# Both score maps of a head issued as one pair, attention spread over 13 and 14 gate units, and three smaller re-orderings in a two-layer backbone kernel

## The chip, the cores and the metric

The kernel runs on one core of one Trainium2 chip. The metric is the device time of one execution in microseconds (us), of which the kernel before has three timed runs. One further execution was recorded by the hardware profiler, and all rows below are from that one.

## The reference

A trunk of two layers works on 256 latent tokens and 256 context tokens of width 1024. Each layer has a mixer (differential attention beside a bidirectional state space, each gated, merged and projected) and a squared-ReLU MLP, both with RMSNorm ahead and behind. Cut to what the change touches:

```python
def diff_attend(q, k, v, lam):                    # two softmax maps per head
    s = einsum('bqhcd,bkhcd->bhcqk', q, k) * (HEAD_DIM_A ** -0.5)
    p = softmax(s, axis=-1)
    pd = p[:, :, 0] - lam * p[:, :, 1]            # their difference weights the values
    return einsum('bhqk,bkhe->bqhe', pd, v)

def trunk_layer(x, xc, ...):
    h = rmsnorm(x, norm_g[0]) * (1 + sc1) + sh1
    q, k, v, u, g = split(h @ w_in)               # latent q sees context and latent keys
    pa = (rmsnorm(latent_diff_attention(q, k_all, v_all, lam), subln_g) * (1 - lam_init)) @ w_br_a
    y_lat, y_ctx = s5_bidirectional(u, uc, ...)   # scans over tokens, then a readout
    y = gelu(y_lat); ps = (y * sigmoid(y @ w_glu + b_glu)) @ w_br_s
    ga, gs = split(sigmoid(g + gate_b))
    x = x + gt1 * rmsnorm((ga * pa + gs * ps) @ w_out, norm_g[1])
    h2 = rmsnorm(x, norm_g[2]) * (1 + sc2) + sh2
    x = x + gt2 * rmsnorm(square(relu(h2 @ w_mlp1 + b_mlp1)) @ w_mlp2 + b_mlp2, norm_g[3])
    # layer 0 does the same for the context tokens, whose queries see context keys only
```

There are 4 heads of two 64-wide maps with values 128 wide. Everything is float32.

## The kernel before

Layer 0 (L0) carries four tiles of 128 tokens (`nt=512` columns), layer 1 (L1) only the two latent ones (`nt=256`). Weights come in pieces of 512 KB on the DMA queue of SP into five buffers `raw`. ScalarE (ACT) rounds a piece to a high part `whi` (L145), VectorE (DVE) takes the rest as `wlo` (L147), and `mm3` (L151 to L153) multiplies in three matmuls, high by high, high by low and low by high.

**Order.** Each engine works through its own list of instructions in order, and a scheduler writes these lists from the order in the program, from buffers that come free and from ties of "issue order" that the program sets with `after(op, prev)`. While the 16 gate projections `ga` run on TensorE (PE), small work is spread between them: steps of the attention, of the scan, of the adaptive-norm product `ada`. `AJ[L]` says over how many of the gate projections the attention steps are spread. The same loop loads the readout matrices `M` (`mload`) and ends with the first pieces of the readout `y`.

**Attention.** One step takes a token tile and a head. `att1` makes for each of the two maps a score matmul `S` (L951: rows 0 to 63 or 64 to 127 of the array, into one of two banks `bbank`), its row maximum `mx` on DVE (L952) and its exponential on ACT (L954), and then the weighted difference `p` (L959). `att2`, one step later, transposes `p` (`pdt`, L966), copies that to `pdT` on ACT (L968) and multiplies with the values into `o` (L970). `att3` ends a token tile: squares, `rsq`, the scaled `on`, its transposes `ot` (L987), then `of` and `oh`. There are 24 such heads: 8 of 256 keys and 8 of 512 in L0, 8 of 512 in L1.

**Readout.** `ssm_out` builds the kernel matrices `kt` per group chunk and stores them to DRAM (`kd`), from where `M` is read back as overlapping windows (L1077). `ygen` multiplies `U` with `M` and the states `S_...` with `CLs` into `y`. `gelu` transposes `y` (`yt`, L1117), then Square, Tanh and the split into `ygh` (L1130) and `ygl`, which the matmuls `glu` take.

**Ends.** `pa_unit` projects the attention output (`pa`). `tail` ends a sub-layer per token tile: a product `mo`, its sum of squares, the multiply with the gate `g2` (L604), `rsq`, the residual `x` (L621), again sums of squares, `xn` (L634 on ACT, L636 on DVE), and behind the next tile's first matmuls the transposes `ht`.

Of the kernel before, what the change touches and what calls it, by code (L numbers as in the profile page):

```python
# [9 lines left out]
F32 = mybir.dt.float32  # L10
# [4 lines left out]
OP = mybir.AluOpType  # L15
# [23 lines left out]
TL = True  # L39
AJ = [14, 16]  # L40
SJ = [15, 10]
# [36 lines left out]
def trunk(tc, I, out):  # L78
    nc = tc.nc
    ctx = ExitStack()  # L80
    with ctx:
# [53 lines left out]

        nosync = mybir.DependencyInfo(mybir.DependencyClass.NoSync, mybir.DependencyReason.DATA)
        hold = {}

# [191 lines left out]
        def ssm_params(L):  # L330
# [125 lines left out]
            ssmt[L]["cl"] = [dram.tile([128, 8, 2, 128], F32, name=f"cl{L}_{c}") for c in range(4)]  # L456
            ssmt[L]["kd"] = [dram.tile([16, 8, 240], F32, name=f"kd{L}_{c}") for c in range(4)]
            yield
# [60 lines left out]
        def ssm_out(L, c):  # L519
# [12 lines left out]
            for g2, r, j, d in np.ndindex(2, 2, 4, 2):  # L532
# [3 lines left out]
                          start=(r == 0), stop=(r == 1), tile_position=(64 * d, 32 * j))  # L536
            kt = chk.tile([128, 2, 240], F32, name="kt")
            pf, pb_ = (p[:, 0:256].rearrange("p (g n) -> p g n", g=2) for p in pks)
# [7 lines left out]
            for j in range(4):  # L546
                S.dma_start(out=z["kd"][c][:, j:j + 5:4], in_=kt[32 * j:32 * j + 16])
            z["done", c] = True
# [33 lines left out]
        def tail(L, n, load, mm, evac, gg, store, norm, ks, fill, hk=None, before=None):  # L582


            late = None
            for t in range(n):
# [9 lines left out]
                def first(n, lo, hi, ps):  # L596
                    a = evac(t, lo, hi, ps)
                    sumsq(a, ss[:, n:n + 1])
                    if n == 0:
                        V.tensor_scalar(ss[:, 4:5], ss[:, 0:1], 1.0 / D, EPS, op0=OP.mult, op1=OP.add)  # L600
                    else:
                        V.scalar_tensor_tensor(ss[:, 4 + n:5 + n], ss[:, n:n + 1], 1.0 / D, ss[:, 3 + n:4 + n],
                                               op0=OP.mult, op1=OP.add)
                    V.tensor_tensor(a, a, g2[:, v, lo:hi], op=OP.mult)  # L604
                    rt.append((a, slice(lo, hi)))
# [12 lines left out]
                with hp(0):  # L618
# [12 lines left out]
                    for q in range(2):  # L631
                        sl = slice(q * 512, q * 512 + 512)
                        if XNE[q]:
                            A.activation(xn[:, sl], x[:, sl], AF.Copy, scale=r)  # L634
                        else:
                            V.tensor_scalar(xn[:, sl], x[:, sl], r, None, op0=OP.mult)  # L636

# [157 lines left out]
        for L in range(DEPTH):  # L795
# [147 lines left out]
            def att1(t, nk, h):  # L943
                qc = (t - t0) * 128
                mx = small.tile([128, 2], F32, name="mx", tag="mx")
                lsum = small.tile([128, 2], F32, name="lsum", tag="lsum")
                pp = []
                for m in range(2):
                    ps = bbank("S")
                    rr = slice(64 * m, 64 * m + 64)  # L950
                    PE.matmul(ps[:, :nk], qT[rr, h, qc:qc + 128], kT[rr, h, 0:nk], start=True, stop=True)  # L951
                    V.tensor_reduce(mx[:, m:m + 1], ps[:, :nk], axis=AX.X, op=OP.max, negate=True)  # L952
                    p = m2(nk, name="p")
                    A.activation(p, ps[:, :nk], AF.Exp, bias=mx[:, m:m + 1], accum_out=lsum[:, m:m + 1])  # L954
                    pp.append(p)
# [6 lines left out]
            def att2(t, nk, h, p, po):  # L962
# [6 lines left out]
                for j in range(nkt):  # L969
                    PE.matmul(po[:, h * 128:(h + 1) * 128], pd[:, j * 128:(j + 1) * 128],  # L970
                              Vk[:, j, h * 128:(h + 1) * 128], start=(j == 0), stop=(j == nkt - 1))

# [97 lines left out]
            def mload():  # L1070

                while ("done", 3) not in z:
                    pump()
                q = len(Ms)
                M = (slot([1024], name="M") if q == 3 and last else xtile("M"))
                kd = z["kd"][q]
                after(S.dma_start(out=M, in_=bass.AP(tensor=kd.tensor, offset=kd.offset,  # L1077
                                                     ap=[[16, 8], [240, 128], [1, 128]])), hold["raw"])
                Ms.append(M.rearrange("p (g n) -> p g n", g=8))

            def ygen():
# [9 lines left out]
                for b in range(8 // A_):  # L1091
# [3 lines left out]
                    for gi, r, a in np.ndindex(4, 3, A_):  # L1095
                        g = b * 4 * A_ + 4 * a + gi
                        if r == 0:
                            w, mv = U[:, g, 64 - ncol:64], Ms[g // 8][:, g % 8]
                        else:
# [9 lines left out]
            def gelu(bp, tq):  # L1109
# [6 lines left out]
                for t in range(4):  # L1116
                    PE.transpose(pt.rearrange("p (a t c) -> p t a c", a=A_, t=4)[:, t],  # L1117
                                 ysb[0][:, bp, 4 * tq + t].rearrange("p b h -> p (b h)"), ident)

# [36 lines left out]

            def pa_unit(fp):
                u = unit(L, U_GA + 3 * fp)
                for b in range(2):
                    k = 2 * fp + b  # L1160
                    pa = proj(u, lambda j: oh[:, j], lambda j: ol[:, j], 0, nt, kn=4, b=b, name="pa")
                    V.scalar_tensor_tensor(m1(k), m1(k), 1.0, pa[:, :nt], op0=OP.add, op1=OP.mult)

            if last:
                while len(ytasks) > 2:
                    ytasks.pop(0)()
                pump(PY[L])
                pa_unit(0)
                pump(PY[L])
                while ytasks:  # L1170
                    ytasks.pop(0)()
                pa_unit(1)
# [290 lines left out]
```

## Time and profile before

| what | value |
|---|---|
| timed runs | 1302.22 us (median of 3, 1299.68 to 1303.11) |
| the profiled execution's own time | 1297.54 us |
| its span (first to last instruction) | 1295.8 us |
| TensorE (PE) busy | 1227.7 us, 95% |
| VectorE (DVE) busy | 887.0 us, 68% |
| ScalarE (ACT) busy | 565.2 us, 44% |
| mean granted TensorE clock | 0.986 of full speed |
| moved by DMA | 228.62 MB, mean 176 GB/s |

The table is read from the top: how far the span is filled by one engine, then the others. Idle time of PE is 1295.8 less 1227.7, that is 68.1 us in the whole span.

### The profile page before, as it was taken

Reading aid. Unit: us, or ns where it says so; the run is one execution under the profiler, and the core shown is the slowest. Engines: PE = TensorE matmul, PEld = TensorE weight load, DVE = VectorE, ACT = ScalarE, POOL = GpSimd, SP = SyncE. Lnnn points to the kernel's source line nnn. Section 1 sums busy time; section 2 is a strip of 40 time slices with the busy share of each in tenths; the row PEclk is TensorE's granted clock in tenths of the full one; section 3 lists DMA queues with packets and bytes.
Section 4 is the critical chain, followed back from the end, with each engine's and each line's share of the span. In section 5 each row is a group of like instructions: output and inputs, shape, how many; then the busy total and the mean of one; then the engine's idle time right before and its main releaser. Section 6 shows DMA issues by size and latency. Waiting matters only on the chain.

```text
span 1295.8 us, 20541 instructions
## 1 busy us (share of the span) xinstructions
PE 1227.7 (95%) x8028; PEld 994.6 (77%) x8028; DVE 887.0 (68%) x2012; ACT 565.2 (44%) x992; POOL 0.2 (0%) x4
## 2 busy tenths in 40 slices
PE   6989999998899999999999999899997988999997
PEld 4668767666678877888778888786775886999996
DVE  7699888434576847987964456733887567766666
ACT  5423355446343642243232253523454644655453
POOL 0000000000000000000000000000000000000000
PEclk9999999999899999999999999999998999999999
DMA  9533372626743466244453243568527955465552
GB/s 372 203 127 114 117 267 82 174 70 237 267 150 143 156 226 213 83 161 154 171 199 93 81 158 120 190 212 335 184 83 196 345 182 180 171 199 180 190 189 81
DMA packets 76497, 228.62 MB, mean 176 GB/s; under 512 B 15952, under 2 KB 26864, under 8 KB 71920
## 3 DMA queue, kind: packets, MB, share of 16 engines
q1 hardware_dynamic: 68080, 225.21, 50.9%
q10 hardware_dynamic: 8320, 2.10, 0.7%
q8 instruction: 63, 1.03, 0.3%
q14 instruction: 34, 0.28, 0.1%
HBM read 205.29 MB, written 21.99 MB: 175 GB/s over the span
## 4 chain that ended last, share of the span: by engine, by line
PE 79%; DMA 8%; DVE 8%; ACT 3%; issue 1%; SPq 1%; DVEq 0%; ACTq 0%
PE m1p L151 6%; PE m1p L153 6%; PE m1p L152 6%; PE m2p L151 5%; PE m2p L152 5%; PE m2p L153 5%; PE mo L151 3%; PE mo L152 3%; PE mo L153 3%; DMA raw<-in_wts 3%; PE ga L151 3%; PE ga L152 2%; PE ga L153 2%; PE S L951 2%; PE ada L287 2%; DMA M<-kd 1%
## 5 line engine op out<-in xcount | busy, mean ns | idle before, releaser
L147 DVE TENSOR_TENSOR wlo<-raw,whi 128x1024 fp32r<-128x1024 f32 x206 | 251.4, 1222 | 166.8 <-ACT whi L145 162.2
L145 ACT ACTIVATE whi<-raw 128x1024 fp32r<-128x1024 f32 x206 | 217.5, 1060 | 335.9 <-PE m2p L153 99.9
L152 PE MATMUL m1p<-l,whi 128*128 128x512 f32 (+1 forms) x448 | 150.9, 337 | 0.0
L151 PE MATMUL m1p<-h,whi 128*128 128x512 f32 (+1 forms) x448 | 150.9, 337 | 0.0
L153 PE MATMUL m1p<-h,wlo 128*128 128x512 f32 (+1 forms) x448 | 150.8, 337 | 0.0
L152 PE MATMUL m2p<-wlo,hid 128*128 128x512 f32 x288 | 112.6, 391 | 0.0
L151 PE MATMUL m2p<-whi,hid 128*128 128x512 f32 x288 | 112.2, 394 | 0.0
L153 PE MATMUL m2p<-whi,hid 128*128 128x512 f32 x288 | 112.2, 390 | 0.0
L151 PE MATMUL ga<-hh,whi 128*128 128x512 f32 (+1 forms) x256 | 89.3, 349 | 4.5 <-ACT whi L145 4.5
L151 PEld LDWEIGHTS m1p<-h,whi 128*128 128x128 f32 x448 | 84.9, 190 | 10.5 <-issue 1.0
L152 PEld LDWEIGHTS m1p<-l,whi 128*128 128x128 f32 x448 | 84.9, 190 | 9.6 <-issue 0.2
L153 PEld LDWEIGHTS m1p<-h,wlo 128*128 128x128 f32 x448 | 85.0, 190 | 8.8 <-DVE kt L543 0.2
L153 PE MATMUL ga<-hh,wlo 128*128 128x512 f32 (+1 forms) x256 | 88.3, 346 | 0.6 <-DVE wlo L147 0.6
L152 PE MATMUL ga<-hl,whi 128*128 128x512 f32 (+1 forms) x256 | 88.3, 345 | 0.0
L151 PEld LDWEIGHTS m2p<-whi,hid 128*128 128x128 f32 x288 | 53.8, 188 | 13.6 <-issue 3.3
L153 PEld LDWEIGHTS m2p<-whi,hid 128*128 128x128 f32 x288 | 54.1, 188 | 11.2
L152 PEld LDWEIGHTS m2p<-wlo,hid 128*128 128x128 f32 x288 | 54.1, 188 | 10.4
L1282 ACT ACTIVATE hid<-zz 128x512 fp32r<-128x512 f32 (+1 forms) x64 | 33.2, 522 | 65.1 <-DVE zz L1281 65.1
L151 PEld LDWEIGHTS ga<-hh,whi 128*128 128x128 f32 x256 | 49.5, 193 | 15.4 <-issue 5.6
L1320 DVE TENSOR_TENSOR acc<-m2p,acc 128x512 f32<-128x512 f32 x60 | 40.9, 687 | 24.3 <-PE m2p L153 24.3
L153 PEld LDWEIGHTS ga<-hh,wlo 128*128 128x128 f32 x256 | 49.3, 193 | 10.6 <-issue 4.2
L152 PEld LDWEIGHTS ga<-hl,whi 128*128 128x128 f32 x256 | 49.5, 193 | 8.9 <-issue 4.5
(318 smaller groups left out, 2701.4 us busy)
## 6 DMA issues: line engine op xcount, KB each, us to landing
raw<-in_wts SPq DMA_DIRECT2D x227, 512.0 KB
raw<-in_ada_w SPq DMA_DIRECT2D x80, 512.0 KB
adaw<-in_ada SPq DMA_DIRECT2D x8, 1024.0 KB
cl<-CL SPq DMA_DIRECT2D x8, 1024.0 KB
CLs<-cl SPq DMA_DIRECT2D x8, 1024.0 KB
x<-in_x SPq DMA_DIRECT2D x8, 512.0 KB
M<-kd SPq DMA_DIRECT2D x8, 512.0 KB
et<-ET SPq DMA_DIRECT2D x4, 1024.0 KB
```

What stands on the lines that cost most here:

```text
L145: a = A.activation(hi, src, AF.Copy)
L147: after(eng.tensor_tensor(lo, src, f(hi), op=OP.subtract), hold.get("x"))
L151: after(PE.matmul(ps, sh, mh, start=first, stop=False), prev)
L152: PE.matmul(ps, sh, ml, start=False, stop=False)
L153: PE.matmul(ps, sl, mh, start=False, stop=last)
L287: PE.matmul(ps[32 * j:32 * j + 32, :n], cs[:, k, :], raw[:, o:o + n], start=(k == 0), stop=(k == 7))
L951: PE.matmul(ps[:, :nk], qT[rr, h, qc:qc + 128], kT[rr, h, 0:nk], start=True, stop=True)
L1282: A.activation(hi, zz, AF.Copy)
L1320: V.tensor_tensor(acc(ti, half), ps, bias2[:, half * 512:(half + 1) * 512] if grp == 0 else acc(ti, half), op=OP.add)
```

## The change

1. `AJ` goes from [14, 16] to [13, 14]: the attention steps end earlier among the gate projections.
2. In `att1` the two score matmuls of a head stand directly behind each other. The first waits for the last exponential of the head before (a real dependency) and stands behind the last `o` of the head before (issue order).
3. `kt` holds the two group halves interleaved, `kd` has the shape [16, 4, 480], a store writes pieces of 1920 bytes instead of 960, and `M` is read in 512 pieces of 1 KB instead of 1024 of 512 bytes. `y` reads every second element of such a tile.
4. In `tail` the multiply with the gate (L604) of a token tile stands behind the `xn` (L636) of the tile before on DVE.
5. In L1 the two `gelu` tasks stand between the halves b=0 and b=1 of `pa_unit(0)`.

```diff
-AJ = [14, 16]
+AJ = [13, 14]
...
-            ssmt[L]["kd"] = [dram.tile([16, 8, 240], F32, name=f"kd{L}_{c}") for c in range(4)]
+            ssmt[L]["kd"] = [dram.tile([16, 4, 480], F32, name=f"kd{L}_{c}") for c in range(4)]
...
-            kt = chk.tile([128, 2, 240], F32, name="kt")
+            ks = chk.tile([128, 480], F32, name="kt")
+            kt = ks.rearrange("p (n g) -> p g n", g=2)
...
-                S.dma_start(out=z["kd"][c][:, j:j + 5:4], in_=kt[32 * j:32 * j + 16])
+                S.dma_start(out=z["kd"][c][:, j], in_=ks[32 * j:32 * j + 16])
...
-                    V.tensor_tensor(a, a, g2[:, v, lo:hi], op=OP.mult)
+                    after(V.tensor_tensor(a, a, g2[:, v, lo:hi], op=OP.mult), normed)
...
-                            V.tensor_scalar(xn[:, sl], x[:, sl], r, None, op0=OP.mult)
+                            normed = V.tensor_scalar(xn[:, sl], x[:, sl], r, None, op0=OP.mult)
...
-                pp = []
+                pp, pss = [], []
                 for m in range(2):
                     ps = bbank("S")
                     rr = slice(64 * m, 64 * m + 64)
-                    PE.matmul(ps[:, :nk], qT[rr, h, qc:qc + 128], kT[rr, h, 0:nk], start=True, stop=True)
+                    o = PE.matmul(ps[:, :nk], qT[rr, h, qc:qc + 128], kT[rr, h, 0:nk], start=True, stop=True)
+                    if m == 0 and "exp" in hold:
+
+                        tc.add_manual_dep(o.ins, hold["exp"].ins.name, sync, reason="both banks")
+                        after(o, hold.get("o"))
+                    pss.append(ps)
+                for m, ps in enumerate(pss):
                     V.tensor_reduce(mx[:, m:m + 1], ps[:, :nk], axis=AX.X, op=OP.max, negate=True)
                     p = m2(nk, name="p")
-                    A.activation(p, ps[:, :nk], AF.Exp, bias=mx[:, m:m + 1], accum_out=lsum[:, m:m + 1])
+                    hold["exp"] = A.activation(p, ps[:, :nk], AF.Exp, bias=mx[:, m:m + 1], accum_out=lsum[:, m:m + 1])
...
-                                                     ap=[[16, 8], [240, 128], [1, 128]])), hold["raw"])
-                Ms.append(M.rearrange("p (g n) -> p g n", g=8))
+                                                     ap=[[32, 8], [480, 64], [1, 256]])), hold["raw"])
+                Ms.append(M.rearrange("p (j n g) -> p g j n", j=4, g=2))
...
+                    if between and b:
+                        between()
+                    pa = proj(u, lambda j: oh[:, j], lambda j: ol[:, j], 0, nt, kn=4, b=b, name="pa",
+                              prev=hold["yt"] if between and b else None)
...
-                pa_unit(0)
+
+                def gelus():
+                    while ytasks:
+                        ytasks.pop(0)()
+                pa_unit(0, gelus)
```

Each engine has as many instructions as before. What moves is their order; three places of PE's list and one of ACT's follow. A row is line, operation, output and inputs, and the columns of one matmul; "x2" is a row twice in succession.

**PE, a head of 512 keys in L0, before.** The gate projection runs on around it (`ga`), with `ada` work behind:

```order
L153 MATMUL ga<-hh,wlo 128x512
L951 MATMUL S<-kT,qT 128x512
L151 MATMUL ga<-hh,whi 128x512
L951 MATMUL S<-kT,qT 128x512
L152 MATMUL ga<-hl,whi 128x512
L970 MATMUL o<-Vk,pdT 128x128 x4
L153 MATMUL ga<-hh,wlo 128x512
L287 MATMUL ada<-raw,cs 32x256
L966 MATMUL pdt<-ident,p 128x128 x4
```

**The same engine, a head of 512 keys in L0, after** (lines are shifted by the edit: L953 is the score matmul, L978 `o`, L974 `pdt`):

```order
L154 MATMUL ga<-hh,wlo 128x512
L978 MATMUL o<-Vk,pdT 128x128 x4
L953 MATMUL S<-kT,qT 128x512 x2
L974 MATMUL pdt<-ident,p 128x128 x4
L288 MATMUL ada<-raw,cs 32x256 x8
L152 MATMUL ga<-hh,whi 128x512
```

The two scores stood apart and now stand together, behind the `o` of the head before the last and ahead of the `pdt` of the last. Over the whole list, 9 of the 24 heads had their scores side by side before (4 of 256 keys, 5 of 512) and 22 have now; all but the first head of each layer. Newly paired are 3 heads of 256 keys and 10 of 512. Between one pair and the next stand 25 rows or more in L0 from the sixth head on, mostly `ga`, but only `pdt` and `o` between the last two; in L1 there are 17 and 6 rows between three successive pairs, `ada`, `ot`, `pdt` and `o` among them, and 30 or more between the others.

**PE, L0, from the last `ot` of the attention to the readout's fourth bank, before:**

```order
L1101 MATMUL y<-CLs,S_3101 64x128
L987 MATMUL ot<-ident,on 128x128
L1117 MATMUL yt<-ident,ysb 128x2x64 x8
L305 MATMUL ada<-ident,row 128x128 x2
L1101 MATMUL y<-M,U 64x128 x2
L1101 MATMUL y<-CLs,S_3101 64x128 x4
```

**The same engine and place, after,** from the last `pa` ahead of that bank (20 further matmuls of `pa` stand between `yt` and these):

```order
L153 MATMUL pa<-ol,whi 128x512
L154 MATMUL pa<-oh,wlo 128x512
L306 MATMUL ada<-ident,row 128x128 x2
L152 MATMUL pa<-oh,whi 128x512
L153 MATMUL pa<-ol,whi 128x512
L154 MATMUL pa<-oh,wlo 128x512
L1109 MATMUL y<-M,U 64x128 x2
L1109 MATMUL y<-CLs,S_3101 64x128 x4
```

The bank that takes the last `M` stood right behind `yt`; now 25 `pa` matmuls of 512 columns stand ahead of it. The pieces of the other three banks keep their places.

**ACT, the turn of L1 from `y` to `glu`, before.** Each `whi` here rounds a weight piece into a buffer that a `pa` unit must first have read:

```order
L1103 ACTIVATE ysb<-y 128x4x8x16 x2
L145 ACTIVATE whi<-raw 128x1024
L1125 ACTIVATE yw<-yt 128x512 x2
L145 ACTIVATE whi<-raw 128x1024
L1128 ACTIVATE yw<-yw 128x512 x2
L145 ACTIVATE whi<-raw 128x1024
L1130 ACTIVATE ygh<-yg 128x4x128 x2
```

**The same engine and place, after:**

```order
L1111 ACTIVATE ysb<-y 128x4x8x16 x2
L1133 ACTIVATE yw<-yt 128x512 x2
L146 ACTIVATE whi<-raw 128x1024
L1136 ACTIVATE yw<-yw 128x512 x2
L146 ACTIVATE whi<-raw 128x1024
L1138 ACTIVATE ygh<-yg 128x4x128 x2
L146 ACTIVATE whi<-raw 128x1024
```

Each of the three `whi` stood ahead of a step of the GELU and now stands behind it; the one that waits for the last `pa` unit is behind `ygh`. On PE the eight `yt` stand behind 12 `pa` matmuls instead of 25, so 60 instead of 47 follow them ahead of `glu`.

Three smaller moves: in L1's `tail` DVE has the first tile's `xn` (L636) ahead of the second tile's two multiplies with the gate; in L1's gate projections `ot` of the first tile stands 1 us of work behind the last `o` instead of 32 `ga` matmuls; and the small loads `ab` and `gr` on SP stand behind five weight loads instead of ahead of them.

## Rows read from the trace of the kernel before

**Rows 1.** The page: the chain that ended last, share of the span by engine.

```profile
PE 79%; DMA 8%; DVE 8%; ACT 3%; issue 1%; SPq 1%; DVEq 0%; ACTq 0%
```

**Rows 2.** PE's waits: engine, instruction, releaser: us in total, times, longest.

```profile
PE y L1101 <- DMA M<-kd: 5.5, 1, 5.5
PE ga L151 <- ACT whi L145: 4.5, 2, 4.2
PE o L970 <- ACT pdT L968: 3.4, 3, 1.7
PE glu L151 <- ACT ygh L1130: 2.1, 1, 2.1
...
PE ot L987 <- ACT on L983: 1.7, 2, 1.4
...
PE S L951 <- ACT p L954: 0.5, 1, 0.5
```

**Rows 3.** Timeline of PE in L0 (start us, us, engine, line): a single score.

```profile
225.00 1.12 PE L951 MATMUL S<-kT,qT 64*128 64x512 f32 x2
226.06 0.50 PE L152 MATMUL ga<-hl,whi 128*128 128x512 f32 x1
```

**Rows 4.** Timeline in L0: a pair of scores (x4) and its chain.

```profile
218.06 1.13 PE L951 MATMUL S<-kT,qT 64*128 64x512 f32 x4
219.12 0.71 PE L970 MATMUL o<-Vk,pdT 128*128 128x128 f32 x4
...
221.15 0.69 ACT L954 ACTIVATE p<-S,mx 128x512 f32<-128x512 f32 x1
...
222.92 0.75 DVE L959 SCALAR_TENSOR_TENSOR p<-p,lsum 128x512 f32<-128x512 f32 x1
```

**Rows 5.** Timeline of PE in L0: a single score of 256 keys.

```profile
141.62 0.70 PE L951 MATMUL S<-kT,qT 64*128 64x256 f32 x2
142.24 0.50 PE L152 MATMUL v<-wlo,hh 128*128 128x512 f32 x1
```

**Rows 6.** Busy us by stretch: PE, PEld, DVE, ACT, POOL, granted clock, DMA share, GB/s.

```profile
200.00:227.00 27.00, 27.00 (x124) 19.75 (x123) 23.34 (x80) 14.11 (x31) 0.00 (x0) 1.00 0.25 79
321.00:328.00 7.00, 1.54 (x12) 1.23 (x14) 4.95 (x11) 3.46 (x7) 0.00 (x0) 0.79 0.98 274
328.00:335.00 7.00, 7.00 (x56) 4.38 (x53) 1.83 (x2) 1.58 (x2) 0.00 (x0) 0.73 0.76 279
984.00:997.00 13.00, 8.53 (x44) 6.04 (x44) 6.79 (x19) 3.83 (x8) 0.00 (x0) 0.74 0.97 271
1049.00:1056.00 7.00, 5.57 (x32) 5.37 (x33) 2.85 (x5) 2.18 (x4) 0.00 (x0) 0.76 0.31 106
```

**Rows 7.** Timeline around L0's last `M`: its issue on SP, then two readouts.

```profile
308.52 0.61 SPq L1077 DMA_DIRECT2D M<-kd  x1
...
317.20 0.44 PE L1101 MATMUL y<-M,U 128*64 128x128 f32 x4
317.47 0.38 PE L1101 MATMUL y<-CLs,S 128*64 128x128 f32 x2
```

**Rows 8.** Matmuls on `U`, forward (L897) and reversed (L898): ns min/median/max.

```profile
L897 PE MATMUL V<-U,ET x128: 221/222/369, 81.9 to 141.1; 128*64 128x64 f32 x128
L898 PE MATMUL V<-U,ET x128: 222/222/369, 81.9 to 141.1; 128*64 128x64 f32 x128
```

**Rows 9.** Timeline of ACT at L1's turn, with what ended the idle time.

```profile
1044.48 1.06 ACT L145 ACTIVATE whi<-raw 128x1024 fp32r<-128x1024 f32 x1 [1.71 <-PE pa L152]
...
1047.37 1.06 ACT L145 ACTIVATE whi<-raw 128x1024 fp32r<-128x1024 f32 x1 [0.78 <-PE pa L152]
1048.33 1.13 ACT L1130 ACTIVATE ygh<-yg 128x512 fp32r<-128x512 f32 x2
```

**Rows 10.** Timeline of DVE in L1's tail.

```profile
1098.33 0.69 DVE L604 TENSOR_TENSOR mo<-mo,gg 128x512 f32<-128x512 f32 x1
...
1100.06 0.48 DVE L636 TENSOR_SCALAR xn<-x,rsq 128x512 f32<-128x512 f32 x1
```

More of the change, by code (lines that the diff above doesn't have):

```diff
@@ L136, in trunk @@
         nosync = mybir.DependencyInfo(mybir.DependencyClass.NoSync, mybir.DependencyReason.DATA)
+        sync = mybir.DependencyInfo(mybir.DependencyClass.Sync, mybir.DependencyReason.DATA)
         hold = {}
@@ L582, in tail @@
         def tail(L, n, load, mm, evac, gg, store, norm, ks, fill, hk=None, before=None):
-            late = None
+            late = normed = None
             for t in range(n):
@@ L969, in att2 @@
                 for j in range(nkt):
-                    PE.matmul(po[:, h * 128:(h + 1) * 128], pd[:, j * 128:(j + 1) * 128],
-                              Vk[:, j, h * 128:(h + 1) * 128], start=(j == 0), stop=(j == nkt - 1))
+                    hold["o"] = PE.matmul(po[:, h * 128:(h + 1) * 128], pd[:, j * 128:(j + 1) * 128],
+                                          Vk[:, j, h * 128:(h + 1) * 128], start=(j == 0), stop=(j == nkt - 1))
             def att3(t, po):
@@ L1097, in ygen @@
                         if r == 0:
-                            w, mv = U[:, g, 64 - ncol:64], Ms[g // 8][:, g % 8]
+                            w, mv = U[:, g, 64 - ncol:64], Ms[g // 8][:, g % 8 // 4, g % 4]
                         else:
@@ L1116, in gelu @@
                 for t in range(4):
-                    PE.transpose(pt.rearrange("p (a t c) -> p t a c", a=A_, t=4)[:, t],
-                                 ysb[0][:, bp, 4 * tq + t].rearrange("p b h -> p (b h)"), ident)
+                    hold["yt"] = PE.transpose(pt.rearrange("p (a t c) -> p t a c", a=A_, t=4)[:, t],
+                                              ysb[0][:, bp, 4 * tq + t].rearrange("p b h -> p (b h)"), ident)
                 def part(x):
@@ L1154, in trunk, with pa_unit @@
             run(at)
-            def pa_unit(fp):
+            def pa_unit(fp, between=None):
                 u = unit(L, U_GA + 3 * fp)
@@ L1160, in pa_unit @@
                     k = 2 * fp + b
-                    pa = proj(u, lambda j: oh[:, j], lambda j: ol[:, j], 0, nt, kn=4, b=b, name="pa")
+                    if between and b:
+                        between()
+                    pa = proj(u, lambda j: oh[:, j], lambda j: ol[:, j], 0, nt, kn=4, b=b, name="pa",
+                              prev=hold["yt"] if between and b else None)
                     V.scalar_tensor_tensor(m1(k), m1(k), 1.0, pa[:, :nt], op0=OP.add, op1=OP.mult)
@@ L1167, in trunk @@
                 pump(PY[L])
-                pa_unit(0)
+                def gelus():
+                    while ytasks:
+                        ytasks.pop(0)()
+                pa_unit(0, gelus)
                 pump(PY[L])
-                while ytasks:
-                    ytasks.pop(0)()
                 pa_unit(1)
```

## The prediction

> **What bounds the kernel now.** I read the page first. The chain that ended last lies on TensorE for 79%, on DMA and DVE for 8% each, on ACT for 3% [rows 1]. So time comes off in two ways: PE does less, or one of its waits falls away. Then PE's own waits: one of 5.5 us for the last `M` of layer 0, 4.5 for a weight's high part, 3.4 in three waits of `o` for `pdT`, 2.1 of `glu` for `ygh` [rows 2]. Then the timeline around the scores, and the busy time by stretch, where the granted clock stands at full 1.00 (2.4 GHz) in the busy stretch from 200 and averages 0.73 to 0.79 in stretches behind or around a wait [rows 6]; it has two levels there, 1.2 and 2.4 GHz, so each such wait is paid a second time.
>
> **The scores.** A single score of 512 keys uses 64 of 128 array rows, starts at 225.00, and the next matmul starts at 226.06: 1.06 us [rows 3]. A pair starts at 218.06 and the `o` behind it at 219.12: again 1.06 us, for two [rows 4]. The two run side by side, so a second score directly behind the first is free, and one that stands apart costs its whole 1.06. For 256 keys a single takes from 141.62 to 142.24, 0.62 us [rows 5]; I take its second score as free too. The order shows 10 heads of 512 keys and 3 of 256 newly paired: 10 x 1.06 + 3 x 0.62 = 12.5 us less on PE. All of it is on the path where PE is what is waited for. A score between two `ga` also disturbs their row a little (0.50 us for the matmul behind it [rows 3]); leaving out 13 such places gives at most about 0.1 us each, 1.3. So 12.5, bounds 12 and 14.
>
> What the pairing adds is a wait: the first score stands behind the last exponential of the head before, and behind that score on PE stand `pdt`, `o` and `ga`, the whole stream. From the pair at 218.06 the second exponential ends at 221.15 + 0.69 = 221.84 and `p` at 222.92 + 0.75 = 223.67, so 3.78 and 5.61 us after its start [rows 4]. Less the 1.06 of the pair itself, PE needs 2.7 us of other work to find both banks free. The `pdt` behind the next pair finds `p` when other work and that pair together fill 5.61 - 1.06 = 4.55, so when the work between is 3.5 us. Where 25 rows or more stand between two pairs, mostly matmuls of the 0.22 us that they take on average (27.00 us for 124 [rows 6]), that is 5.5 us: nothing waits. Between the last two pairs of L0 stand only `pdt` and `o`. There a wait was already there before (0.5 us of `S`, the only one it has [rows 2]); new is that `o` stands directly behind `pdt` and no score covers the copy to `pdT`. The three waits of that kind were 3.4 us [rows 2], 1.1 each: +1.2 for it, bounds 0.5 and 2.
>
> **Layer 1's middle.** Here `ot` moves to 1 us behind the last `o`, so its wait for `on` (1.7 us in all before [rows 2]) grows by the 32 `ga` that no longer cover it; at 256 columns I estimate them at half of 0.22, so 3.5 us: +2.5 to +3.5. But those 32 `ga` now stand behind the `ada` work that frees the weight buffers, where PE waited 4.2 us in one piece for a `whi` [rows 2] and lost more to the clock: 13 us at 0.74 are 3.4 us, in part idle [rows 6]. The wait moves from `whi` to `ot`, and the half clock may move along. Two of the pairs here have little between them. I take 0, bounds -4 and +4. That `ab` and `gr` stand later on SP lets weights be issued earlier, but their buffers are freed by the same `ada` matmuls, so I credit nothing.
>
> **The readout of layer 0.** The last `M` was issued at 308.52 [rows 7] and PE waited for it for 5.5 us, with the DMA engines 0.98 busy from 321 to 328 [rows 6], so it is late from transfer. Behind it 7 us ran at 0.73, which costs 0.27 x 7 = 1.9 us [rows 6]; 5.5 + 1.9 = 7.4. Now 25 `pa` of 512 columns, 0.22 us each and 5.5 together, fill the place in which PE stood. That covers the wait if the transfers keep their times. But PE comes here earlier by what the scores save, while the transfers go on at their rate, so some of it stays, and other loads (`CLs`, `ada` weights) are near. I take 5.5 of the 7.4 that wait and clock cost; bounds 2 and 7.4.
>
> **Pieces of 1 KB, and the stride.** Half as many pieces could shorten only that late transfer; it is 0.5 MB of what ran at 274 GB/s, so 1.9 us if alone, and it is part of the wait already counted: 0, lower bound -1. The price could be `y`, which now reads every second element. Four such matmuls start at 317.20 and the next at 317.47, 0.27 us [rows 7]; 128 records are 8.6 us, and reading at half speed would add as much. The nearest row is `V`, whose `U` is read forward and reversed at the same 222 ns [rows 8]. Reading backward is no stride, yet it shows that order alone costs nothing. I take 0, upper bound +8.6. The stores are as many as before, of longer pieces, and `kt` is written interleaved by a few small DVE operations per chunk, while PE has projections to do: 0.
>
> **The turn of layer 1.** The `whi` that waits for the last `pa` ran from 1047.37, and `ygh` behind it from 1048.33 [rows 9]: `glu` waited 2.1 us [rows 2]. In the 7 us from 1049 PE is idle for 1.43, of which at most 0.5 is that wait's end, and the clock at 0.76 takes 1.7 [rows 6]. Together 2.1 + 0.9 + 1.7 = 4.7. Now `ygh` stands ahead of that `whi`, behind the one that waited until 1044.48 only, which ends at 1045.54; and `yt` comes 13 `pa` of 256 columns earlier, 1.4 us. The Tanh between needs its two DVE steps, so `ygh`, which ended at 1049.46, could end at about the last `pa`, 1047.4. I take 4.0 of 4.7, bounds 2 and 4.7.
>
> **The tails.** In L1 a multiply of 0.69 us stood at 1098.33 amid the first tile's chain, whose `xn` came at 1100.06 [rows 10]. Two of them now wait behind `xn`, which brings the first tile forward by perhaps 0.6 us and puts the second back by as much. L0's tails keep their order on PE. I take 0, bounds -0.6 and +0.6.
>
> **The sum.** -12.5 + 1.2 + 0 - 5.5 + 0 - 4.0 + 0 = -20.8. Against the profiled execution's own 1297.5 that is 1276.7, a ratio of 0.984; that execution lies 0.36% below the median of the timed runs, 1302.2, and the ratio on this gives 1281.3. The bounds of the terms, not all at one end, give this case 1273 to 1289.
>
> **The rivals.**
> - *The pairs are paid back.* DVE is busy for 23.3 of 27 us from 200 on [rows 6], 86%. If PE gets 1.06 us faster per head there, the maxima and `p` come later against it, and each pair finds its banks still taken. For it: that share, and that the scan runs on DVE in the same stretch. Against: one wait of 0.5 us for `S` in the whole trace [rows 2]. If half of the 22 pairs wait for 0.7 us, 7.7 come back: 1289. The Trainium skill, "TensorEngine Tiling (Array Packing)", section "Gotcha 1: PSUM Pressure", says that row tiles go to different banks and that software must see to it, so that a pair needs two banks at once. This speaks against the change, since `bbank` has just two, and a kernel that issues singles can use one bank as it comes free; the trace has nine pairs before and bears out only that two run at once. By that page the time would be this rival's, 1289.
> - *The pairs make it slower.* Each pair of 512 keys waits for the second exponential and PE then falls to the half clock. 22 pairs at 1.1 us wait are 24 us, against 12.5 gained; with the other terms (-9.5 and +1.2) the time is 1305.6, and with a half clock behind every third of them, 1.7 us each as at the turn, 1318. It decides when the waits reach 1.0 us a pair, that is when work between pairs falls below 1.7 us by the 2.7 worked out above. Order speaks against it everywhere but at three places.
> - *Only the pairs work.* The late `M` just shifts with PE's earlier arrival, `glu` waits for something else, and L1's middle costs 3: -12.5 + 1.2 + 3 - 1 = -9.3, so 1293.
> - *The stride costs double.* +8.6 on the forecast: 1290.
> - *More goes away.* All of `M`'s and `glu`'s waits with their half clock, and L1's `whi` wait: -14 + 0.5 - 4 - 7.4 - 4.7 = -29.6, so 1273.
> - *Nothing happens,* because what PE saves is given back at the next weight load, since 16 `ga` cannot end before their weights: 1302, within 0.3%. The weights wait for buffers that PE itself frees, so I do not believe it.
>
> **How the numbers follow.** Forecast 0.60; pairs paid back 0.12; only the pairs 0.08; the stride 0.03; more goes away 0.06; nothing 0.05; slower 0.06. No change is what lies within 0.3%, that is 3.9 us, about what this kernel's timing can tell. All but the last two are faster, 0.89 together; 0.03 of that I give to no change, for cases that are paid back further than their rival says. So 0.86, 0.08 and 0.06. The range goes from 1270 to 1295: it holds the forecast's own 1273 to 1289, the three cases from 1289 to 1293 and most of the case with more gain, and leaves out no change and slower.
>
> **What would show it.** Right: PE's busy time for `S` (L953) falls by about 12 us and two start within 0.02 us of each other in 22 heads; no wait of `y` for `M` above 2 us; `glu` waits under 1 us; clock at 1.00 behind both. Wrong: waits of `S` for `p` in many heads; `pdt` waiting for `p`; `y` at 0.54 us per four records; a `whi` wait in L1 of more than 4 us besides a wait of `ot` above 4.

## The result and the profile after

The changed kernel takes 1280.88 us (median of 4 runs, 1277.56 to 1283.69) against 1302.66 us of the kernel before on the same chips: a ratio of 0.983, 95% interval 0.980 to 0.986. The forecast was 1281, range 1270 to 1295. The profiled execution took 1279.62 us, 17.9 us less than that of before. Executions of one kernel differ, and their granted clock with them: those of the kernel before that were timed beside e9 go from 1296.54 us at a mean clock of 0.984 to 1308.52 at 0.972, and the profiled one, 1297.54 at 0.986, is among the fastest, so that differences of traces come out smaller than those of medians.

So the number was met. Whether for the reasons given is another matter. PE's own work first, in the page of the changed kernel (busy us, share, instructions):

```profile
PE 1213.3 (95%) x8028; PEld 989.4 (77%) x8028; DVE 887.9 (69%) x2012; ACT 564.9 (44%) x992; POOL 0.2 (0%) x4
```

PE is busy for 14.4 us less than before, DVE and ACT for as long. The pairs run as [rows 4] had shown, in a timeline of PE in layer 0 (start us, us, engine, line, xcount):

```profile
213.08 0.60 PE L978 MATMUL o<-Vk,pdT 128*128 128x128 f32 x4
213.62 1.13 PE L953 MATMUL S<-kT,qT 64*128 64x512 f32 x4
214.68 0.44 PE L974 MATMUL pdt<-ident,p 128*128 128x128 f32 x2
```

Two scores take 1.06 us together, and with 22 heads paired PE is busy on that line for 25.96 us instead of 40.13 on the same line of before. In the view of that line no score waits for an exponential any more; what ended the idle time before the scores is

```profile
its engine sat idle before it (us, times) until:
  issue: 2.1, 7
  ACT Vt L903: 0.4, 1
```

The wait that the pairs bring is not at the score. PE's waits (us in total, times, longest), to be held against [rows 2]:

```profile
PE ht L644 <- DVE xn L638: 6.9, 2, 5.0
PE ada L288 <- DMA raw<-in_ada_w: 6.3, 5, 2.3
PE ot L995 <- ACT on L991: 4.8, 1, 4.8
...
PE o L978 <- ACT pdT L976: 2.9, 3, 2.2
...
PE pdt L974 <- DVE p L967: 2.1, 2, 1.2
PE ada L288 <- DVE row L296: 2.0, 1, 2.0
```

The first two rows were much the same before, 6.0 us for `ht` and 5.7 for `raw`. `y` no longer waits for `M`, `glu` no longer for `ygh`. In their place `ot` waits 4.8 us in one piece (1.4 before). `pdt` waits 2.1 us for `p` (0.5 before), and the adaptive product 2.0 (1.3 before) until DVE has read its one bank into `row`.

To see where time went I cut the profiled executions at five starts on PE that all kernels have, which gives four stretches: the first score of layer 0 (before 141.62, after 141.64), the last `mo` of its first sub-layer (440.41, 427.58), the first score of layer 1 (904.08, 892.06), the last `pa` of layer 1 (1060.78, 1043.68) and the last `mo` of all (1287.68, 1269.77). The differences to the kernel before, in us, with those of all experiments, and the ratio of the timed runs:

| kernel | L0 mixer | L0 MLP to L1's projections | L1 mixer | rest | ratio, 95% interval |
|---|---|---|---|---|---|
| changed | -12.9 | +0.8 | -5.1 | -0.8 | 0.983 (0.980 to 0.986) |
| e1 without pairs | -8.8 | -0.1 | -5.0 | -0.6 | 0.986 (0.982 to 0.991) |
| e2 old turn | -10.9 | +1.3 | -1.0 | -0.6 | 0.989 (0.984 to 0.994) |
| e3 old pieces | -8.9 | +2.5 | -8.1 | -0.6 | 0.986 (0.981 to 0.990) |
| e4 late `ot` | -12.1 | +3.1 | -7.1 | -0.6 | 0.984 (0.980 to 0.987) |
| e5 spread alone | -6.4 | +0.9 | +0.7 | -0.4 | 0.994 (0.991 to 0.997) |
| e6 pairs alone | -2.8 | +2.0 | -0.6 | -0.4 | 0.994 (0.992 to 0.997) |
| e7 no tail order | -11.7 | +2.6 | -4.9 | -0.4 | 0.984 (0.980 to 0.988) |
| e8 late `ada` | -12.5 | -0.3 | -12.2 | -0.4 | 0.979 (0.975 to 0.983) |
| e9 pieces alone | -2.5 | +1.1 | +0.9 | -0.3 | 0.995 (0.992 to 0.997) |
| e10 e8 without pairs | -8.2 | +2.5 | -4.3 | +0.9 | 0.987 (0.982 to 0.992) |
| e11 other `ada` places | -10.7 | +3.7 | -7.6 | -0.4 | 0.981 (0.977 to 0.986) |
| e12 e8 with early `M` | -12.1 | +2.9 | -17.4 | -0.6 | 0.977 (0.973 to 0.980) |

The stretch ahead of the first score is left out; it differs from before by -1.8 (e1) to +3.3 us (e12). In the second column little of the change acts, and it still goes from -0.3 to +3.7. The other columns scatter too, from one execution to the next: e2, e4, e8, e11 and e12 have the changed kernel's order on PE all through L0's mixer and lie between -10.7 and -12.5 there, where the changed kernel has -12.9; e3 has its order throughout and takes 3.0 us less in L1's mixer. So differences of about 2 us in the first column, and of 3 to 4 in the next two, are not read as an edit's without a wait that shows them, nor are ratios whose intervals overlap.

### The profile page after: what moved, and what is told of

The parts are those of the page before. It is cut to its first block, busy times and chain, and to the rows that moved or that the text cites. A ratio compares the mean times of both kernels' runs of the same rounds, so it can differ in the third digit from the quotient of the medians.

```text
span 1277.8 us, 20549 instructions
## 1 busy us (share of the span) xinstructions
PE 1213.3 (95%) x8028; PEld 989.4 (77%) x8028; DVE 887.9 (69%) x2012; ACT 564.9 (44%) x992; POOL 0.2 (0%) x4
## 4 chain that ended last, share of the span: by engine, by line
PE 79%; DVE 9%; DMA 8%; ACT 3%; issue 1%; SPq 0%; DVEq 0%; ACTq 0%
PE m1p L152 6%; PE m1p L153 6%; PE m1p L154 6%; PE m2p L152 5%; PE m2p L153 5%; PE m2p L154 5%; DMA raw<-in_wts 4%; PE mo L152 3%; PE mo L153 3%; PE mo L154 3%; PE ada L288 3%; PE ga L154 3%; PE ga L152 3%; PE ga L153 3%; PE S L953 1%; DMA raw<-in_ada_w 1%
## 5 line engine op out<-in xcount | busy, mean ns | idle before, releaser
L288 PE MATMUL ada<-raw,cs 128*32 128x256 f32 (+1 forms) x576 | 52.7, 441 | 9.0 <-DMA raw<-in_ada_w 6.3
```

The lines of the kernel that those rows point to most:

```text
L288: PE.matmul(ps[32 * j:32 * j + 32, :n], cs[:, k, :], raw[:, o:o + n], start=(k == 0), stop=(k == 7))
```

## The experiments

**e1: without the pairs.** The tie and the second loop are taken out of the changed kernel; in its trace 7 heads have their scores side by side instead of 22.

```diff
-                    if m == 0 and "exp" in hold:
-                        tc.add_manual_dep(o.ins, hold["exp"].ins.name, sync, reason="both banks")
-                        after(o, hold.get("o"))
-                    pss.append(ps)
-                for m, ps in enumerate(pss):
```

> The changed kernel without the tie on the score matmuls and with the old loop (scores, maximum and exponential map by map); everything else as changed. 8 heads are paired in its list of PE, not 22. Theory (a score that stands apart costs PE its whole 1.06 us, 0.62 us with 256 keys): 14 heads fall apart again, so PE is busy some 12 us longer and the time is 1.0% above the changed kernel, ratio to the kernel before about 0.993. Rival (pairs are mostly paid back because DVE is the bound in the stretches of attention): the time rises by 5 us or less, ratio about 0.987, and PE's idle time falls.

Measured: PE's busy time rises as the theory says, in the page

```profile
PE 1226.1 (96%) x8028; PEld 990.6 (77%) x8028; DVE 887.2 (69%) x2012; ACT 565.2 (44%) x992; POOL 0.2 (0%) x4
```

by 12.8 us. The time does not: 1283.12 us, and in the table the pairs are worth 4.1 us in layer 0 (12.9 less 8.8) and 0.1 in layer 1. The term of 12.5 us was right as work and wrong as time. The intervals of the two ratios overlap, so this is read from the trace, the mixers of L0 and L1 (columns as in [rows 6]). The changed kernel:

```profile
141.64:427.58 285.94, 277.63 (x1690) 208.41 (x1683) 190.97 (x528) 140.26 (x289) 0.00 (x0) 0.99 0.53 173
892.06:1043.68 151.62, 136.56 (x1099) 115.28 (x1098) 113.61 (x322) 80.94 (x151) 0.00 (x0) 0.93 0.65 203
```

e1:

```profile
139.82:429.83 290.01, 286.92 (x1691) 209.47 (x1683) 190.86 (x528) 140.64 (x289) 0.00 (x0) 1.00 0.51 170
893.38:1045.10 151.72, 140.74 (x1100) 115.82 (x1098) 112.74 (x322) 80.90 (x151) 0.00 (x0) 0.97 0.66 204
```

In L0 the pairs take 9.3 us off PE's work and add 5.2 us of idle time (8.3 against 3.1); in L1 they take off 4.2 and add 4.1. The 4.1 us of L0 are beyond the scatter: all six kernels with the changed kernel's order there lie 1.9 to 4.7 us below e1 and e10. For L1 the table gives no more than a value near 0, give or take 3.

**e2: the turn as before.**

```diff
-                pa_unit(0, gelus)
+                pa_unit(0)
                 pump(PY[L])
+                gelus()
```

> The changed kernel with the two gelu tasks of layer 1 behind the whole of pa_unit(0) again. On PE only the eight yt move, 13 rows later, on ACT one whi moves ahead of Tanh. Theory (ygh stands behind the whi that waits for the last pa): glu waits 2 us for ygh again and about 1 us for ygl, with some 1.7 us of half clock behind it, 3 to 4.7 us in all, ratio about 0.987. Rival (the gain of the turn came with the earlier end of attention, not with the place of yt): glu waits under 1 us as in the changed kernel, no difference.

Measured: 1286.03 us. The wait is back, with its own rows, and the stretch behind it (columns as in [rows 6]):

```profile
PE glu L152 <- ACT ygh L1138: 2.1, 1, 2.1
...
PE glu L153 <- DVE ygl L1139: 0.9, 1, 0.9
```

```profile
1040.00:1047.00 7.00, 5.62 (x44) 5.42 (x45) 3.81 (x6) 3.08 (x6) 0.00 (x0) 1.00 0.30 98
```

The mechanism holds. But the clock stays at 1.00 behind the wait, where [rows 6] had 0.76 behind the same wait; so it is 2.3 us of trace between the last `y` and the last `pa` (21.8 against 19.5, and 23.3 in the kernel before), not 4. The other 1.7 us by which this run's L1 mixer is behind the changed kernel's arose earlier, where the adaptive product waited 3.5 us for a weight's transfer instead of 2.1.

**e3 and e9: the pieces, taken back and alone.** e3 is the changed kernel with the old `kd`, `kt`, `M`; e9 is the kernel before with the new ones, the five lines of the diff above on `kd`, `kt`, `ks`, `M` and `Ms`.

> The changed kernel with kd, kt, M and y as before: 512-byte pieces, y reads neighbouring elements. No engine's order changes. Theory (pieces and stride cost and bring nothing to be seen, since 25 pa now stand in front of the last M of layer 0): same time within 1.5 us, records of y<-M of 273 ns in both, no wait of y for M above 0.5 us. Rival 1 (the larger pieces removed the wait): y waits for M again, 2 to 5 us. Rival 2 (the stride costs): y<-M records shorter here and up to 8 us less.

> The kernel before with the larger pieces of kd and M alone; the order on PE, DVE and ACT is that of the kernel before. Theory now (the stores of kt, not the loads of M, are what the pieces change: the one buffer kt waits 4.3 us in three waits for its stores, each store takes SP 590 ns to issue, and the ada weights of layer 0's attention are queued behind them): kt waits about 2 us, an issue takes about 410 ns, the first ada weights are issued some 2.5 to 3 us earlier than at 160.3, and 1.5 to 3 us of it are still there at the end of layer 0's attention; ratio 0.998. The 5.5 us wait for the last M stays within 1.5 us. Rival (as I had forecast): no difference to be seen before that M, and it comes 1 us earlier at most.

Measured: 1282.84 us and 1296.58 us. The matmuls `y<-M` take a median of 273 ns from neighbouring and of 276 ns from every second element, so the stride costs nothing to be seen. In e3 `y` does not wait for `M` either: the pieces were not what removed that wait. But the whole first stage is 4.0 us shorter with the new pieces (1.8 at least, against the other kernels with that order), and 2.5 us in e9, where no engine's order differs from before. The lead of e9 is there by 173 us of its trace, and so the cause stands at the head of the attention. Before: the stores on SP's queue, `kt`'s wait for them on DVE, and the load queued behind them

```profile
L547 SPq DMA_DIRECT2D kd<-kt x32: 548/590/1544, 134.1 to 682.1; - x32
...
DVE kt L539 <- DMA kd<-kt: 4.3, 3, 2.0
...
160.25 1.95 SPq L283 DMA_DIRECT2D raw<-in_ada_w  x4
```

and in e9:

```profile
L548 SPq DMA_DIRECT2D kd<-kt x32: 302/416/1527, 133.9 to 678.7; - x32
...
DVE kt L540 <- DMA kd<-kt: 1.9, 2, 1.5
...
156.91 2.49 SPq L283 DMA_DIRECT2D raw<-in_ada_w  x5
```

A store of 16 x 1920 bytes takes SP 416 ns to issue instead of 590, the one buffer `kt` is free sooner, and the adaptive weights for which PE waits next are issued 3.3 us earlier. That these stores are the cause is read from the two traces (the changed kernel and e3 differ in the same way: 413 ns and 2.2 us against 589 ns and 4.3 us); no run has the stores alone. The last `M` of layer 0 was waited for 4.9 us instead of 5.5: the forecast's part of this edit was the smaller one. Not all of the gain lasts: at the end of its trace e9 is 1.0 us ahead of the kernel before, the rest went in layer 1's projections.

**e4: `ot` of layer 1's first tile behind the next step's `o`.**

```diff
-                pt = tbank("ot")
-                for h in range(NH):
...
-                    PE.transpose(pt[:, hs], on[:, hs], ident)
...
+                def fin():
+                    pt = tbank("ot")
+                    for h in range(NH):
...
+                        tr = PE.transpose(pt[:, hs], on[:, hs], ident)
+                        if h == 0:
+                            after(tr, hold["o"])
...
                         att2(t, nk, h, p, po)
+                        if fin is not None:
+                            fin()
...
```

> The changed kernel, but in layer 1 the first tile's transposes ot stand behind the next step's o instead of right behind the last head's. In the changed kernel PE waits 4.8 us there for `on`, and 7 us behind run at half clock. Theory (PE stands for nothing else there): that wait goes, and with it 2 to 3.5 us of half clock, 4 to 7 us less, ratio about 0.979. Rival (DVE, 6.6 of 7 us busy there with the scan, is the bound, and the weights behind come late): the wait moves to pdt, the adaptive row or a whi, and the time stays within 2 us.

Measured: 1279.80 us, no difference, as the rival said. The wait moved to the next thing in the list:

```profile
PE ada L306 <- DVE row L304: 5.5, 1, 5.5
```

What stands there in the changed kernel, on PE, DVE and ACT of layer 1's middle:

```profile
955.72 1.13 PE L953 MATMUL S<-kT,qT 64*128 64x512 f32 x4
961.65 1.25 PE L995 MATMUL ot<-ident,on 128*128 128x128 f32 x4 [4.80 <-ACT on L991]
```

```profile
957.68 0.16 DVE L986 TENSOR_SCALAR sso<-sso 128x4 f32<-128x4 f32 x1
...
961.04 0.15 DVE L252 SCALAR_TENSOR_TENSOR rsq<-rsq 128x4 f32<-128x4 f32 x1
```

```profile
961.22 1.14 ACT L991 ACTIVATE on<-o,rsq 128x128 f32<-128x128 f32 x4 [3.84 <-DVE rsq L252]
```

The sum of squares is there at 957.68, the root 3.5 us later, since most of its small steps on DVE have a step of the scan or a maximum between them and the next. `on` waits for it at the head of ACT's list, and behind `on` stand the copies and exponentials that the next `pdt`, `o` and `ada` on PE need. The order tried here does not help, and the reading is that PE needs work that hangs on none of them; e8 tests it.

**e5 and e6: the spread alone and the pairs alone,** on the kernel before (`AJ = [13, 14]`; and the new `att1` with the ties).

> The kernel before with AJ [13, 14] alone. Undoing the pairs in the changed kernel cost only about 2 us of median although PE's scores cost 10 us more, and the 5.5 us wait of y for the last M did not come back. Theory now (the spread, not the place of yt or the pairs, took the wait for M: the readout of layer 0 comes with pa in front): the time is 8 to 11 us below the kernel before, ratio 0.992 to 0.994, no wait of y for M in layer 0 above 1 us, glu still waits 2 us. Rival (the pairs or the pieces took it): the wait of 5.5 us stays and the ratio is 0.998 or more.

> The kernel before with the paired scores alone (AJ [14, 16], old pieces, tail and turn). Theory by the forecast's term: PE's scores fall by about 10 us and nearly all of it is seen, ratio 0.991. Rival, which the run without pairs speaks for: waits of ada, pdt, o and ot take back most of it, ratio 0.996 to 1.0, and the sum of PE's idle time rises by 6 us or more.

Measured: 1294.39 and 1294.89 us. For e6 that is between its theory (ratio 0.991) and its rival (0.996 or more). In both, `y` never waits for the last `M`: either edit alone makes the scheduler put `pa` in front of that bank, so the gain of this wait, 6.4 us of the first stage in e5, is there once and not twice. The pairs alone gain 2.8 us in that stage, less than the wait that they too removed: the scores' 7 us of layer 0 are paid back, among others at `pdT` (3.4 us before) and `row` (1.3 before). The `ot` is layer 1's, and `glu` waits as it did before:

```profile
PE o L977 <- ACT pdT L975: 5.1, 5, 2.2
PE ot L994 <- ACT on L990: 4.8, 1, 4.8
...
PE ada L288 <- DVE row L296: 2.5, 1, 2.5
PE glu L152 <- ACT ygh L1137: 2.1, 1, 2.1
```

So the wait of 4.8 us at `ot` comes with the pairs: e6 has it, while e1 waits 0.8 us there and e5 0.9.

**e7: without the order in the tail.**

```diff
-                    after(V.tensor_tensor(a, a, g2[:, v, lo:hi], op=OP.mult), normed)
+                    V.tensor_tensor(a, a, g2[:, v, lo:hi], op=OP.mult)
```

> The changed kernel without the order of the gate multiply in tail. Theory (in layer 1 xn of the first tile comes about 0.6 us earlier by that order and that of the second as much later): from the last mo of layer 1's first sub-layer to the end it takes 0 to 1 us longer here, which the medians can't tell; the scheduler moves 61 rows of PE's list elsewhere, so a larger difference is not the tail's. Rival: the wait of ht for xn is 1.5 us longer here and the ratio rises to 0.985.

Measured: 1282.10 us, not to be told from the changed kernel. In layer 1's tail `ht` waits 6.0 us here for the first tile and 5.0 there, and for the second tile 1.2 here and 1.9 there: 0.3 us in all (0.4 in the table), inside what was worked out ahead for that edit (0, bounds 0.6).

**e8, e10, e11, e12: layer 1's middle covered.** `PG` says how many adaptive steps follow a gate projection, `MJ` at which of them an `M` is loaded.

```diff
-PG = [(0, 0, 1, 1), (1, 1, 1, 1)]
+PG = [(0, 0, 1, 1), (0, 1, 1, 1)]
```

e10 is the same with the pairs taken out as in e1. e11 instead puts two steps behind the second gate projection:

```diff
-PG = [(0, 0, 1, 1), (1, 1, 1, 1)]
+PG = [(0, 0, 1, 1), (0, 2, 1, 1)]
```

and e12 adds to e8's line

```diff
-MJ = [(11, 12, 13), (0, 4, 8)]
+MJ = [(11, 12, 13), (0, 2, 4)]
```

> The changed kernel with no step of the adaptive product during the first four gate projections of layer 1 (PG 0 for 1): between the first tile's last o and its ot stand 60 ga matmuls now. Theory (the 4.8 us wait of ot is the chain squares, rsq, on, with DVE full of scan steps, which any other PE work would cover; moving ot alone did not help since the adaptive row stands behind on in ACT's list): waits of ot and of the row go, and with them half clock, 4 to 8 us less, ratio about 0.978 to 0.980. Rival (weights are late there, and ada that comes later holds their buffers): waits of ga for whi or of ada for raw take the place, ratio 0.983 or more.

> The best kernel so far (adaptive product later in layer 1, 1274.7 us) without the tie that pairs the scores. Theory (in the changed kernel layer 1's five new pairs were worth 5.3 us on PE and were paid back by the wait of ot that the pairs' order uncovered; with that wait covered the pairs count in full): layer 1's mixer takes 4 to 6 us longer than with pairs and the whole 6 to 9 us longer, ratio 0.984 to 0.986. Rival (pairs are paid back in layer 1 wherever they stand, since DVE with the scan and the weights set the pace): 2 to 4 us longer as in the changed kernel, ratio 0.981.

> The changed kernel with PG (0, 2, 1, 1) in layer 1: no adaptive step in the first four gate projections and two in each of the next four. Between the first tile's last o and its ot stand 28 ga matmuls, about 3.1 us, and the adaptive product comes nearly as early as in the changed kernel. Theory (the chain from o to on takes 6.7 us from the end of o: squares, rsq amid the scan, on): 28 ga leave 2 to 3 us of the 4.8 us wait, but the weights behind come earlier than in the run with 60, where ga waited 3.8 us for a whi and y 2.8 us for M; about the same as that run, ratio 0.978 to 0.981. Rival: two adaptive steps in succession hold all weight buffers and ga waits above 4 us, ratio 0.983 or more.

> The best kernel so far (adaptive product later in layer 1) with the loads of M at gate projections 0, 2 and 4 of layer 1 instead of 0, 4 and 8, so that they go while the DMA engines are 0.32 busy (955 to 970 there). In that run y waited 2.8 us for M and ga 3.8 us for a whi, with the clock at 0.52 over the 10 us behind. Theory (these two waits are the rest of the price of the late adaptive product, and both are transfers queued together): the wait for M goes, that for whi falls by 1 to 2 us, 3 to 5 us less, ratio 0.974 to 0.977. Rival (the whi is late from the buffers that ada holds, not from the transfers, and takes all of the place): ratio 0.978 to 0.981.

Measured: e8 1274.72 us, e10 1287.13, e11 1280.11, e12 1272.80. In e8 60 `ga` stand between a pair of scores and `ot`, which now waits for nothing (timeline of PE):

```profile
956.19 1.13 PE L953 MATMUL S<-kT,qT 64*128 64x512 f32 x4
...
964.53 0.27 PE L995 MATMUL ot<-ident,on 128*128 128x128 f32 x1
...
972.10 0.63 PE L974 MATMUL pdt<-ident,p 128*128 128x128 f32 x4 [1.29 <-DVE p L967]
```

L1's mixer is 7.1 us shorter than in the changed kernel (12.2 less 5.1), as its theory said; the intervals of the two ratios overlap. The price is later, a weight and an `M` behind the adaptive loads, with the clock near its lower level:

```profile
PE ga L152 <- ACT whi L146: 3.8, 1, 3.8
PE y L1109 <- DMA M<-kd: 2.8, 1, 2.8
```

```profile
955.00:970.00 15.00, 14.75 (x116) 13.15 (x114) 13.13 (x59) 8.85 (x28) 0.00 (x0) 1.00 0.32 109
...
980.00:990.00 10.00, 4.89 (x27) 3.86 (x28) 4.83 (x16) 3.49 (x7) 0.00 (x0) 0.52 0.99 284
```

e10 tests what the pairs are worth when the wait they uncover is covered: 7.9 us of layer 1's mixer (12.2 less 4.3), where they were worth 0.1 in the changed kernel. That is clear of the scatter, and more than the 5.3 us of their work and the 4 to 6 expected; the two lists differ in more than the pairs, so the surplus is not explained. e11 leaves a wait of 1.3 us at `ot` and one of 3.4 for an `M`, and comes out between the changed kernel and e8, which its interval does not tell from either. e12 moves that `M` of e8 to where the DMA engines were 0.32 busy. Its wait for the `whi` ends at 988.16, that of e8 at 982.33, so the same stretch is here

```profile
986.00:996.00 10.00, 7.84 (x65) 6.17 (x66) 6.06 (x18) 5.90 (x10) 0.00 (x0) 0.83 0.82 302
```

with no wait for `M`. The `whi` is still 4.1 us late, as the rival said of it, and the ratio is at the upper end of the theory's. e12 has the lowest ratio of the study, 0.977 (0.973 to 0.980) against 0.983 (0.980 to 0.986) of the change; its interval does not tell it from e8's, and its profiled execution was no shorter (1273.76 us against 1272.12), so what e12 adds to e8 is shown for that wait and not for the whole.

## Why the prediction was right, and where its steps were not

The change was read rightly in kind (less work for the scores, no wait for the last `M`, a shorter turn), and the signs named for it came: two scores start within 0.01 us of each other in 22 heads, `y` waits for no `M`, and the clock is at 1.00 behind the readout and behind the turn. One of the signs against it came too, `pdt` waiting for `p`. That the sum came out is in part luck. Term by term, forecast against what the stages show:

| term | forecast | measured | from |
|---|---|---|---|
| scores of layer 0, with the wait for `pdT` | -6.0 | -4.1 | changed less e1 |
| scores of layer 1 and its middle | -5.3 | -0.1 | changed less e1 |
| the last `M` of layer 0 | -5.5 | -6.4 | e5 |
| pieces and stride | 0 | -2.5 | e9 |
| the turn | -4.0 | -4.0, of which 2.3 its own | changed less e2 |
| the tails | 0 | -0.4 | changed less e7 |
| sum | -20.8 | -17.5 | profiles; -17.9 found, and -21.8 in the medians |

Two terms were too large, by 7.1 us together, and two too small, by 3.4. The forecast lies 2.9 us from what the traces show. It lies 1.0 us from the medians because it was worked out from an execution of the kernel before that was 5.1 us faster than the median (1297.54 against 1302.66), while the profiled one of the changed kernel was 1.3 us faster than its own. The prediction gives no reason why these should make up for its terms, so the hit to within 1 us is luck. Single terms under 2 us are within the scatter of the stages.

**The scores.** "All of it is on the path" failed. PE does 12.8 us less (e1), as priced from [rows 3] and [rows 5], but the tie fixes `o`, the pair and `pdt` in a row, and what stood between them as cover is gone. PE's waits in L0's mixer of the changed kernel:

```profile
PE o L978 <- ACT pdT L976: 2.5, 2, 2.2
PE ada L288 <- DVE row L296: 2.0, 1, 2.0
PE y L1109 <- ACT p L962: 1.0, 1, 1.0
PE ga L154 <- DVE wlo L148: 0.9, 1, 0.9
PE pdt L974 <- DVE p L967: 0.9, 1, 0.9
```

In e1 the `row` takes 0.9 us there, the `p` the same 0.9, and the other three are gone. I had tested the wait of the score itself against 2.7 us of work, and none came; of the `pdt` against 3.5, one new wait came, 1.2 us in layer 1. The price of `o` behind `pdt`, put at 1.2, was 2.2 in one piece, and the `row` and `y` were not looked at. I had also put the old wait of 0.5 us for `S` between the last two pairs of L0; it stood in layer 1:

```profile
996.37 1.79 PE L951 MATMUL S<-kT,qT 64*128 64x512 f32 x4 [0.53 <-ACT p L954]
```

The rival that the pairs are paid back was given 0.12 and is nearer to what the pairs did than the forecast's term. But the cause that it gave is not what the runs show: no score waited for one of the two banks, and only `y`, which takes the same banks, waited 1.0 us for an exponential.

**Layer 1's middle.** "I take 0" was the weakest step. I had seen that `ot` loses its 32 `ga` and that its wait grows by 2.5 to 3.5, and set against it that the wait for a `whi` would go by as much. Both came with about that size, `ot` from 1.4 to 4.8 us and the `whi` from 4.2 to 0.8. But the step left out what came besides: ahead of the weights there were still a wait of 0.8 for a `wlo` and one of 2.1 for an adaptive piece, `pdt` waited 1.2 for `p`, and the clock was at 0.50 and 0.57 in two stretches:

```profile
962.00:969.00 7.00, 6.32 (x44) 3.22 (x43) 6.23 (x26) 4.17 (x11) 0.00 (x0) 0.50 0.23 54
...
976.00:983.00 7.00, 4.89 (x29) 3.79 (x30) 3.55 (x14) 2.47 (x5) 0.00 (x0) 0.57 0.97 319
```

Over L1's mixer the granted clock averaged 0.93 (e1: 0.97), against 0.97 before:

```profile
904.08:1060.78 156.70, 141.34 (x1099) 116.31 (x1098) 113.19 (x322) 80.61 (x151) 0.00 (x0) 0.97 0.62 199
```

With the turn's 4.0 and pairs of 5.3 the L1 mixer should have lost 9.3 and lost 5.1, so the middle cost 4.2: just beyond the upper end of the bound that the forecast had set, not its middle.

**The last `M`.** Right in place, and in size as far as the stage of e5 tells. The cover is the 25 `pa`, and the wait is gone in every kernel that has either the spread or the pairs (e3, e5, e6), not in e9, which has neither. That both edits give the same gain was not seen.

**The pieces.** "0" failed for a reason that the trace of before showed and I did not look up: the wait of `kt` for its own stores and SP's time for their issue, ahead of loads that PE waits for. I had priced the load of `M` and the matmuls, and put the stores at nothing since DVE's part of them is small. The -2.5 is that of the stage; 1.0 of it was left at the end of e9.

**The turn.** The mechanism was right, its clock was not: 1.7 of the 4.7 us were taken from one stretch at 0.76, and e2, e6 and e9 have the same wait of 2.1 us with the clock at 1.00 behind it. Between the last `y` and the last `pa` those three take 21.8 us and the kernel before 23.3, so the half clock cost that one execution 1.5 us.

**The tails and the stride** came out at nothing, as said.

## What to carry to other kernels

Work saved on the busiest engine counts only where its list keeps cover behind each short chain: before the saving is credited, go through the new list for each consumer that now stands right behind its producer's other half, on ACT and DVE too. If two edits each remove the same wait, credit it once. And where a store's buffer is written again soon, price the store by its issue and by its queue's next load, not by its bytes.

## What the runs showed of the hardware

The same wait of PE, 2.1 us for `ygh` and 0.9 for `ygl` after a full stretch, was followed by a granted clock of 0.76 over 7 us in one execution and of 1.00 in three others. In e6 and e9, the columns as in [rows 6]:

```profile
1049.00:1056.00 7.00, 5.49 (x43) 5.29 (x44) 3.82 (x6) 3.16 (x7) 0.00 (x0) 1.00 0.32 101
```

```profile
1050.00:1057.00 7.00, 5.76 (x45) 5.55 (x46) 3.81 (x7) 2.89 (x6) 0.00 (x0) 1.00 0.26 85
```

In e5 the wait was longer, 4.0 us for `ygh` in one piece, and the half clock was there again:

```profile
1046.00:1053.00 7.00, 6.80 (x45) 6.79 (x46) 2.65 (x5) 2.75 (x6) 0.00 (x0) 0.76 0.21 72
```

So a half clock read behind one wait of 2 to 3 us is not a price that comes back with it each time. And a store from 16 partitions to DRAM was issued in 590 ns with 32 pieces of 960 bytes and in 416 ns with 16 of 1920.
